# Second-half tokens turned by VectorE block transposes while they are normalized, and reloaded as channel-major rows

## The chip, the cores and the metric

The kernel runs on one core of one Trainium2 chip. The metric is the device time of one execution in microseconds (us); lower is better. TensorE is called PE below, VectorE DVE, ScalarE ACT, GpSimd POOL and SyncE SP, as in the profile.

## The reference

One layer of a hybrid decoder trunk for a sequence of 2048 tokens of 1024 channels, with 16 learned meta tokens put ahead of them. `h` is the RMS norm of the tokens, `p = h @ w_in` one projection to 8208 columns. Eight heads run a gated delta rule, and 1024 channels run a gated short convolution; both results are concatenated and projected back.

```python
def hybrid_layer(x, norm_g, w_in, ...):
    h = rmsnorm(x, norm_g)
    p = h @ w_in
    qkv, dn_z, dn_a, dn_b, sc_b, sc_c, sc_h, sc_z = jnp.split(p, SPLITS, axis=-1)
    qkv = jax.nn.silu(causal_dwconv(qkv, dn_conv_w))
...
    o = chunk_gated_delta_rule(q, k, v, g, beta)
    o = rmsnorm(o, dn_out_g) * jax.nn.silu(dn_z)
    y = sc_b * causal_dwconv(sc_c * sc_h, sc_conv_w)
    o_sc = y * jax.nn.silu(sc_z)
    return x + jnp.concatenate([o_dn, o_sc], axis=-1) @ w_out
```

The output is the RMS norm of the layer's result without the meta tokens.

## The kernel before, in words

**Halves.** The tokens are worked off in two halves of 1024. For each half the normalized tokens stand channel-major in two tiles, `hh` (`HH`, rounded to fp32r) and `hl` (`HL`, the rest), [128 channels, 8 channel groups, 1040 tokens]. There is one pair for both halves: a token tile of the second half (128 tokens) overwrites `hh` and `hl` when the last two projection jobs of the first half have passed those columns.

**Jobs.** A job (`run_group`, line 750) is one block of 128 output columns: 24 matmuls for each group of tokens (hh by wh, hl by wh, hh by wl), into the PSUM tile `mm`. The first half has three groups (272, 384 and 384 tokens), the second two of 512. A job's result is drained by ACT (`raw` and `acc` for the convolution of q, k and v) and finished by DVE (`acc<-raw,pcol,acc`). The weights of a later job are loaded by SP, rounded by ACT (`wh<-wr`), and their rest taken by DVE (`wl<-wr,wh`); for two jobs at the seam of the halves POOL takes the rest.

**Order.** PE, ACT, DVE and POOL run a fixed order written when the program is built. Jobs run one after the other; beside them run generators (streams) for the delta rule. A stream yields an amount of time, and `pump` (line 234) resumes it when a simple clock, kept by class `Model`, has passed that. So a stream's instructions fall between the matmuls of whatever job is running. Where a job needs something a stream has not delivered, `require` (line 257) advances the clock without emitting matmuls until the stream has. Engines run their lists strictly in order, and wait for one another by semaphores.

**A head.** For head `i` (0 to 7 in the first half, 8 to 15 in the second) `delta_front` (line 975) builds the blocks and runs a triangular substitution on DVE (`prod`, `XT`; `msm`, `mXT` for the meta tokens), `delta_back` (line 1124) merges blocks on PE (`ta`, tiles `Q`, `X`, `W`), and `delta_scan` (line 1304) runs eight chunks. Each chunk has three steps on PE, each waiting for the one before through another engine:

```python
mmf(pr[:, :128], lhsT=k_[:, c, :], rhs=S)        # rec<-S,k, then o<-S,qd
nc.vector.scalar_tensor_tensor(y, pr[:, :128], ...)   # DVE yy
mmf(pv[:, :128], lhsT=W[:, c, :], rhs=y)         # rec<-yy,W
nc.scalar.activation(vn, pv[:, :128], ...)       # ACT vn
mmf(pS[:, :128], lhsT=kd[:, c, :], rhs=vn)       # rec<-vn,kd, then o<-vn,P
nc.vector.scalar_tensor_tensor(Sn, S, ...)       # DVE S, then the next chunk
```

`delta_back(i)` waits for `("fresh", i)` and for scan `i - 1`. A job for k of head `i` needs scan `i - 2` (`pre_k`, line 830), a job for q needs the blocks of head `i - 2` (`pre_q`, line 836).

**The second half's tokens.** They are prepared during the first half. `normalize(t)` (line 526) loads tile t into `kd`, loads `norm_g` into the places of `Q` and `gw` (both held against other users meanwhile), takes the mean square on ACT and POOL, scales `kd` on DVE in two pieces of 128x512 and stores 512 KB to the DRAM tile `xnd`. It runs inside the stream `fresh(i)` (line 1079), after scan `i - 1`: one tile for heads 0 to 4 and 6, two for head 5. At the end of the first half `prologue1` (line 556) loads the eight tiles back into `sc_c`, `sc_y`, `sc_u`, and `turn` (line 391) does for each half tile four PE transposes into a PSUM tile `ta`, an ACT copy to `hh` and a DVE subtraction to `hl`. `LANDING` (line 1395) is the clock time given to a load.

## Time and profile before

| | |
|---|---|
| median of 3 runs | 2226.82 us (2225.97 to 2227.2) |
| the profiled execution, its own time | 2231.35 us |
| its span, first to last instruction | 2229.6 us |
| mean granted PE clock | 0.99 |
| busy share of the span | PE 98%, weight loads 86%, DVE 65%, ACT 38%, POOL 9% |
| DMA, mean over the span | 88 GB/s, 46% of the 16 engines' time |

The profile is of one execution. Views show the busy time of each engine in a stretch, the time that one engine waited for another, the instructions in order of time, and groups of equal instructions. A line is named by engine, operation, and output<-inputs with their sizes; all instructions stand at L118, the helper that records them, so tiles tell them apart. Transposes on PE are shown as MATMUL with `ident` as an input. A granted clock of 1.00 is 2.4 GHz, 0.50 is 1.2 GHz.

### The profile page before, as it was taken

To read this page: it belongs to the slowest core of one execution; us is meant where nothing else is said; L and a number is where in the kernel's file an instruction comes from. 1 tells how busy PE (TensorE), PEld (TensorE's weight loads), DVE (VectorE), ACT (ScalarE), POOL (GpSimd) and SP (SyncE) were. 2 spreads that over 40 slices of the span, in tenths; PEclk is the share of its full clock that TensorE was granted. 3 is DMA by queue.
4 is the path that set the end of the run, shared out by engine and by line. 5 is a ranking of instruction groups with operands and counts; after the bars stand their busy time and mean duration, and the time that the engine had idled before them with its cause. 6 is when DMAs were issued, how large, how long until landed. Compare 5 with 4: busy or idle time off the path is not lost.

```text
span 2229.6 us, 35449 instructions
## 1 busy us (share of the span) xinstructions
PE 2176.5 (98%) x13472; PEld 1917.2 (86%) x13472; DVE 1454.9 (65%) x3911; ACT 851.3 (38%) x1991; POOL 195.8 (9%) x361
## 2 busy tenths in 40 slices
PE   6999999999999999999999999999999999999998
PEld 5999999999999999878888888888878887788886
DVE  4677777777777777776767767676657683444222
ACT  5533434343434444443434352434342533322111
POOL 4010101010101010201010110010000100000000
PEclk9999999999999999999999999999989998999999
DMA  5434444353548844534254424353846443645321
GB/s 141 82 79 67 84 72 94 64 97 60 100 56 108 88 88 62 131 54 77 55 78 54 82 51 87 50 83 65 66 37 73 88 118 114 212 157 188 114 90 57
DMA packets 257096, 196.26 MB, mean 88 GB/s; under 512 B 61957, under 2 KB 226318, under 8 KB 256926
## 3 DMA queue, kind: packets, MB, share of 16 engines
q1 hardware_dynamic: 256926, 194.00, 46.0%
q8 instruction: 106, 1.74, 0.3%
q14 instruction: 64, 0.52, 0.1%
HBM read 157.89 MB, written 36.06 MB: 87 GB/s over the span
## 4 chain that ended last, share of the span: by engine, by line
PE 92%; DMA 2%; DVE 2%; ACT 2%; issue 1%; SPq 0%; POOLq 0%; ACTq 0%; DVEq 0%
PE mm L118 78%; PE ta L118 7%; PE rec L118 4%; PE o L118 3%; DMA wr<-in_w_in_dram 1%; ACT junk L118 1%; SPq L118 0%; DVE prod L118 0%; DVE hl L118 0%; DMA xtd<-XT 0%; DMA wr<-mixd 0%; DMA ysd<-raw 0%; DVE XT L118 0%; DVE acc L118 0%; ACT hh L118 0%
## 5 line engine op out<-in xcount | busy, mean ns | idle before, releaser
L118 PE MATMUL mm<-hh,wh 128*128 128x512 f32 (+3 forms) x2816 | 1006.3, 365 | 10.2 <-ACT hh L118 8.6
L118 PE MATMUL mm<-hl,wh 128*128 128x512 f32 (+3 forms) x2816 | 986.2, 358 | 0.2 <-DVE hl L118 0.2
L118 PE MATMUL mm<-hh,wl 128*128 128x512 f32 (+3 forms) x2816 | 641.4, 360 | 4.6 <-DVE wl L118 4.6
L118 PEld LDWEIGHTS mm<-hh,wh 128*128 128x128 f32 x2816 | 532.0, 190 | 61.5 <-ACT hh L118 9.8
L118 PEld LDWEIGHTS mm<-hl,wh 128*128 128x128 f32 x2816 | 531.9, 189 | 47.5 <-DVE hl L118 1.1
L118 PEld LDWEIGHTS mm<-hh,wl 128*128 128x128 f32 x2816 | 480.7, 189 | 53.6 <-DVE wl L118 5.5
L118 DVE TENSOR_TENSOR wl<-wr,wh 128x512 fp32r<-128x512 f32 x348 | 230.5, 685 | 69.3 <-ACT wh L118 34.1
L118 DVE SCALAR_TENSOR_TENSOR acc<-raw,pcol,acc 128x384 f32<-128x384 f32 (+2 forms) x360 | 231.3, 644 | 50.3 <-ACT acc L118 42.5
L118 ACT ACTIVATE wh<-wr 128x1024 fp32r<-128x1024 f32 x178 | 187.9, 1056 | 133.8 <-PE mm L118 88.1
L118 DVE SCALAR_TENSOR_TENSOR prod<-nb,XT 128x8 f32<-128x8 f32 (+30 forms) x496 | 194.3, 392 | 11.2 <-DMA nb<-nbd 6.4
L118 DVE TENSOR_REDUCE XT<-prod 128x8 f32<-128x16 f32 (+30 forms) x496 | 147.3, 297 | 17.1
L118 ACT ACTIVATE raw<-mm 128x384 f32<-128x384 f32 (+2 forms) x120 | 61.7, 514 | 227.8 <-PE mm L118 227.7
L118 ACT ACTIVATE vn<-rec,cj 128x128 f32<-128x128 f32 x128 | 46.9, 367 | 219.2 <-PE rec L118 218.8
L118 ACT ACTIVATE sc_c<-mm 128x384 f32<-128x384 f32 (+3 forms) x82 | 42.3, 516 | 176.1 <-PE mm L118 169.7
L118 PE MATMUL mm<-oh,wh 128*128 128x512 f32 x256 | 101.9, 398 | 0.0
L118 PE MATMUL mm<-ol,wh 128*128 128x512 f32 x256 | 100.4, 392 | 0.0
L118 DVE SCALAR_TENSOR_TENSOR yy<-rec,neg,vr 128x128 f32<-128x128 f32 x128 | 44.6, 349 | 71.6 <-PE rec L118 70.8
L118 DVE TENSOR_TENSOR y<-mm,y 128x512 f32<-128x512 f32 x23 | 15.9, 692 | 111.4 <-PE mm L118 111.4
L118 ACT ACTIVATE ojk<-y 128x512 bf16<-128x512 f32 x23 | 14.5, 631 | 183.4 <-DVE y L118 127.2
L118 POOL TENSOR_TENSOR opy<-mo,nhalf 128x4 f32<-128x4 f32 x32 | 33.7, 1052 | 509.4 <-DVE mo L118 509.4
L118 ACT ACTIVATE acc<-mm,pcol 128x384 f32<-128x384 f32 (+2 forms) x120 | 72.1, 601 | 0.1
L118 DVE SCALAR_TENSOR_TENSOR S<-S,egl,rec 128x128 f32<-128x128 f32 x104 | 35.8, 344 | 53.8 <-PE rec L118 53.5
(242 smaller groups left out, 2530.3 us busy)
## 6 DMA issues: line engine op xcount, KB each, us to landing
wr<-in_w_in_dram SPq DMA_DIRECT2D x128, 512.0 KB, 7.9
wr<-mixd SPq DMA_DIRECT2D x50, 512.0 KB, 4.5
E<-gtd SPq DMA_DIRECT2D x16, 512.0 KB, 3.8
qd<-ged SPq DMA_DIRECT2D x16, 512.0 KB, 3.9
nb<-nbd SPq DMA_DIRECT2D x64, 128.0 KB, 4.4
mixd<-zs SPq DMA_DIRECT2D x32, 256.0 KB, 2.4
out_dram<-y SPq DMA_DIRECT2D x16, 512.0 KB, 2.6
kd<-in_x_dram SPq DMA_DIRECT2D x9, 512.0 KB, 9.8
```

Of the source, the lines that this page charges most:

```text
L118: r = real(*args, **kw)
```

## The change

`normalize` does more. After each half tile of 128x512 is scaled, `turn_out` transposes its 32x32 blocks on DVE (one `STREAM_TRANSPOSE`, 128x512) into the place of the gain just used (`Q`, then `gw`), and four DMAs store it to `xnd`, which is now laid out by channel group, channel, token. Each writes rows of 32 elements (128 bytes) and 64 KB in all, so that the blocks land in their transposed positions. Then the stream yields `DRAIN` (4.0 on the order's clock) before `Q` and `gw` are let go and tile t is marked ready.

`prologue1` loads a tile as [128 channels, 8 groups, 128 tokens], rows of 512 bytes. `turn` with its PE transposes and its PSUM tile is gone; `split_h` copies from SBUF on ACT and subtracts on DVE, and the stream no longer waits for a `ta` slot.

```diff
-    xnd = tc.dram_tile([NC, 128, D], F32, name="xnd")
+    xnd = tc.dram_tile([NC, KT, 128, 128], F32, name="xnd")
...
-    def turn(xt, k0, col, n):
...
-            tr(pt[:, k, :n], xt[:, kx * 128 : kx * 128 + 128], n)
...
+    def split_h(xt, k0, col):
+        x_ = xt[:, 512 * k0 : 512 * k0 + 512].rearrange("p (k i) -> p k i", i=128)
+        h_ = HH[:, 4 * k0 : 4 * k0 + 4, col : col + 128]
+        l_ = HL[:, 4 * k0 : 4 * k0 + 4, col : col + 128]
+        nc.scalar.activation(h_, x_, AF.Copy)
+        nc.vector.tensor_tensor(out=l_, in0=x_, in1=h_, op=ALU.subtract)
...
             nc.vector.scalar_tensor_tensor(xc, xc, rs, gains[c2], op0=ALU.mult, op1=ALU.mult)
+            turn_out(
+                xnd[i, 4 * c2 : 4 * c2 + 4],
+                xc.rearrange("p (c i) -> p c i", i=128),
+                gains[c2].rearrange("p (c i) -> p c i", i=128),
+            )
+            yield after(eng="DVE", lag=0.3)
+        yield DRAIN
         held.discard("Q")
         held.discard("gw")
-        nc.sync.dma_start(xnd[i], xt)
...
-            nc.sync.dma_start(xts[i], xnd[i])
+            nc.sync.dma_start(
+                xts[i].rearrange("p (k i) -> p k i", i=128), xnd[i].rearrange("k p i -> p k i")
+            )
...
-                yield after(xts[i], slot=(pta, "ta"), eng="DVE", lag=1.2)
-                yield from hold()
-                turn(xts[i], k0, col, 128)
+                yield after(xts[i], eng="DVE", lag=1.2)
+                split_h(xts[i], k0, col)
...
+    def turn_out(dram, src, tmp):
+        nc.vector.transpose(out=tmp.rearrange("p c i -> p (c i)"), in_=src.rearrange("p c i -> p (c i)"))
+        for a in range(4):
+            nc.sync.dma_start(
+                dram[:, :, 32 * a : 32 * a + 32].rearrange("c (b y) x -> y (c b) x", b=4),
+                tmp[32 * a : 32 * a + 32].rearrange("y c (b x) -> y (c b) x", b=4),
+            )
...
+    DRAIN = 4.0
```

The instruction counts: PE loses 64 transposes, DVE gains 16 transposes, SP gains 56 DMAs (64 stores of 64 KB for 8 of 512 KB). All else is as often as before, but since the streams' yields differ, the instructions of the heads stand elsewhere among the jobs' matmuls. Two places follow.

**The end of head 4's scan, first on PE.** The last steps before, where `mm` rows are the running job:

```order
L118 MATMUL rec<-yy,W 128x128
L118 MATMUL mm<-hh,wh 128x384
L118 MATMUL mm<-hl,wh 128x384
L118 MATMUL mm<-hh,wl 128x384 x6
L118 MATMUL rec<-vn,kd 128x128
L118 MATMUL o<-vn,P 128x128
```

Eight matmuls of the job stood between the last two steps of the last chunk. The same steps on PE now:

```order
L118 MATMUL rec<-vn,kd 128x128
L118 MATMUL o<-vn,P 128x128
L118 MATMUL mm<-hh,wl 128x384 x2
L118 MATMUL rec<-S,k 128x128
L118 MATMUL o<-S,qd 128x128
L118 MATMUL rec<-yy,W 128x128
L118 MATMUL rec<-vn,kd 128x128
L118 MATMUL o<-vn,P 128x128
L118 MATMUL mm<-hh,wh 128x272
```

The chunk has moved back past the end of a job, so that its last two steps follow each other with none of a job's matmuls between them. The same place on ACT now:

```order
L118 ACTIVATE raw<-mm 128x384
L118 ACTIVATE acc<-mm,pcol 128x384
L118 ACTIVATE qcar<-raw 128x3
L118 ACTIVATE wh<-wr 128x1024
L118 ACTIVATE q<-acc 128x384
L118 ACTIVATE vn<-rec,cj 128x128
```

The last `vn` now stands behind the job's drain (`raw`, `acc`) and the rounding of the next weights (`wh`). Head 5 ends in the same way, with eight matmuls ahead of its last `rec<-S,k`.

**The end of head 6's scan, at the seam of the halves, on PE.** Before:

```order
L118 MATMUL rec<-S,k 128x128
L118 MATMUL o<-S,qd 128x128
L118 MATMUL mm<-hh,wl 128x384 x8
L118 MATMUL rec<-yy,W 128x128
L118 MATMUL mm<-hh,wh 128x384
```

These are the steps of the last chunk, inside the first half's last two jobs, with matmuls in every step. On PE now (the rows of 512 columns are the second half's first and second job):

```order
L118 MATMUL mm<-hh,wl 128x512 x5
L118 MATMUL rec<-yy,W 128x128
L118 MATMUL rec<-vn,kd 128x128
L118 MATMUL o<-vn,P 128x128
L118 MATMUL rec<-S,k 128x128
L118 MATMUL o<-S,qd 128x128
L118 MATMUL rec<-yy,W 128x128
L118 MATMUL rec<-vn,kd 128x128
L118 MATMUL o<-vn,P 128x128
L118 MATMUL mm<-hh,wh 128x512
```

The last four steps have moved behind the second half's first job and stand together, with no matmul of a job between them. DVE at this place now:

```order
L118 SCALAR_TENSOR_TENSOR yy<-rec,neg_857,vr 128x128
L118 TENSOR_TENSOR hl<-sc_c,hh 128x4x128
L118 SCALAR_TENSOR_TENSOR prod<-nb,XT 128x8x3
L118 TENSOR_REDUCE XT<-prod 128x8
L118 TENSOR_TENSOR hl<-sc_c,hh 128x4x128
L118 TENSOR_TENSOR hl<-sc_y,hh 128x4x128
L118 SCALAR_TENSOR_TENSOR prod<-nb,XT 128x8x4
L118 TENSOR_REDUCE XT<-prod 128x8
L118 TENSOR_TENSOR hl<-sc_y,hh 128x4x128
L118 SCALAR_TENSOR_TENSOR S<-S,egl,rec 128x128
```

The state `S` that the last chunk starts from has moved behind four subtractions for `hl` of the last two token tiles.

## Rows read from the trace of the kernel before

**Rows 1.** Page, part 1: busy us, share of the span, instructions.
```profile
PE 2176.5 (98%) x13472; PEld 1917.2 (86%) x13472; DVE 1454.9 (65%) x3911; ACT 851.3 (38%) x1991; POOL 195.8 (9%) x361
```

**Rows 2.** Time line of PE in the seam: start us, us, instruction.
```profile
910.25 0.34 PE L118 MATMUL mm<-hl,wh 128*128 128x384 f32 x1
910.43 0.60 PE L118 MATMUL ta<-ident,sc_c 128*128 128x128 f32 x4
910.78 0.42 PE L118 MATMUL mm<-hh,wh 128*128 128x384 f32 x1
911.04 0.33 PE L118 MATMUL mm<-hl,wh 128*128 128x384 f32 x1
```

**Rows 3.** Waits of PE: us in total, times, longest.
```profile
PE ta L118 <- DVE hl L118: 2.2, 2, 1.8
```

**Rows 4.** Windows: stretch, length, busy of PE, PEld, DVE, ACT, POOL; clock.
```profile
625.00:700.00 75.00, 74.95 (x596) 72.02 (x595) 52.52 (x156) 31.36 (x91) 7.50 (x14) 1.00 0.59 72
926.00:946.00 20.00, 16.95 (x93) 13.67 (x92) 19.26 (x61) 10.54 (x25) 8.07 (x8) 1.00 0.49 92
```

**Rows 5.** Time line of PE and ACT at the end of head 0's scan.
```profile
258.03 0.43 PE L118 MATMUL rec<-yy,W 128*128 128x128 f32 x2
...
258.23 0.49 ACT L118 ACTIVATE raw<-mm 128x384 f32<-128x384 f32 x1 [0.44 <-PE mm L118]
...
259.17 1.05 ACT L118 ACTIVATE wh<-wr 128x1024 fp32r<-128x1024 f32 x1
...
260.12 0.37 ACT L118 ACTIVATE vn<-rec,cj 128x128 f32<-128x128 f32 x1
...
260.54 0.49 PE L118 MATMUL rec<-vn,kd 128*128 128x128 f32 x2 [2.08 <-ACT vn L118]
```

**Rows 6.** Time line of two scan steps whose DVE and ACT stood free.
```profile
808.84 0.38 PE L118 MATMUL rec<-S,k 128*128 128x128 f32 x2
...
809.26 0.35 DVE L118 SCALAR_TENSOR_TENSOR yy<-rec,neg,vr 128x128 f32<-128x128 f32 x1 [0.37 <-PE rec L118]
...
810.69 0.38 PE L118 MATMUL rec<-yy,W 128*128 128x128 f32 x2
...
811.17 0.37 ACT L118 ACTIVATE vn<-rec,cj 128x128 f32<-128x128 f32 x1 [2.03 <-PE rec L118]
```

**Rows 7.** Groups of DVE by form: count, busy us, mean ns, idle before.
```profile
L118 DVE STREAM_TRANSPOSE X<-W 32x256 f32<-32x256 f32 x48 | 20.7, 432 | 11.8 <-DMA W<-xtd 10.8
L118 DVE TENSOR_TENSOR hl<-ta,hh 128x512 fp32r<-128x512 f32 x24 | 16.2, 683 | 4.7 <-ACT hh L118 4.4
...
L118 DVE SCALAR_TENSOR_TENSOR kd<-kd,pxr,Q 128x512 f32<-128x512 f32 x8 | 6.0, 752 | 0.4
```

**Rows 8.** Windows as in rows 4, around stalls of PE.
```profile
258.00:260.00 2.00, 0.46 (x4) 0.27 (x2) 1.08 (x6) 1.77 (x4) 0.00 (x0) 1.00 0.73 223
...
1620.00:1625.00 5.00, 4.10 (x41) 2.92 (x44) 3.65 (x7) 0.75 (x2) 0.00 (x0) 0.58 0.07 12
...
1635.00:1640.00 5.00, 5.00 (x21) 4.18 (x20) 1.01 (x2) 0.89 (x2) 0.00 (x0) 0.71 1.02 52
...
1840.00:1845.00 5.00, 1.45 (x5) 0.87 (x5) 2.02 (x4) 1.78 (x4) 0.00 (x0) 0.77 0.31 108
```

**Rows 9.** Time line of PE after a late weight in the output projection.
```profile
1932.91 2.08 PE L118 MATMUL mm<-hh,wl 128*128 128x512 f32 x4 [4.26 <-DVE wl L118]
1934.79 0.63 PE L118 MATMUL mm<-hh,wh 128*128 128x512 f32 x1
...
1938.20 0.44 PE L118 MATMUL mm<-hh,wh 128*128 128x512 f32 x1
...
1940.09 2.00 PE L118 MATMUL mm<-hh,wl 128*128 128x512 f32 x8
```

**Rows 10.** DMA issues: count, KB each, median us to landing.
```profile
wr<-in_w_in_dram SPq DMA_DIRECT2D x128, 512.0 KB, 7.9
...
nbd<-E SPq DMA_DIRECT2D x64, 32.0 KB, 2.4
```

More of the change, by code (lines that the diff above doesn't have):

```diff
@@ L388, in parted @@
         hready[hf, g] = max(model.free["ACT"], model.free["DVE"]) + model.LATENCY
-    def turn(xt, k0, col, n):
-        pt = ptile(pta, "ta", [128, 4, 128])
-        for k in range(4):
-            kx = 4 * k0 + k
-            tr(pt[:, k, :n], xt[:, kx * 128 : kx * 128 + 128], n)
-        h_ = HH[:, 4 * k0 : 4 * k0 + 4, col : col + n]
-        l_ = HL[:, 4 * k0 : 4 * k0 + 4, col : col + n]
-        nc.scalar.activation(h_, pt[:, :, :n], AF.Copy)
-        nc.vector.tensor_tensor(out=l_, in0=pt[:, :, :n], in1=h_, op=ALU.subtract)
+    def split_h(xt, k0, col):
[4 more added lines that the diff above has]
+        nc.vector.tensor_tensor(out=l_, in0=x_, in1=h_, op=ALU.subtract)
     def statistics(xt, n, jk):
```

## The prediction

> **What bounds the kernel now.** I read the busy shares first: PE is busy for 98% of the span, DVE for 65% [rows 1]. So PE's list of instructions sets the time, and only two things change it: matmuls taken from or added to that list, and time in which PE waits. The windows then tell where PE waits: in the middle of the first half it is busy for 74.95 of 75 us, while at the seam of the halves it is busy for 16.95 of 20 us and DVE for 19.26 [rows 4]. There DVE paces PE; one wait there is PE's transposes standing for `hl` to free their PSUM tile, 2.2 us [rows 3]. Last I read the time lines around the places where the change moves instructions. Idle time of DVE, ACT and SP elsewhere costs nothing.
>
> The sum is made against the profiled execution, 2231.35 us, whose span is 2229.6. The median of the runs is 2226.82, 4.5 lower, so I add the difference to the median. About 0.2%, 4.5 us, is what a measurement of this kernel can tell from no change.
>
> **The change, part by part.**
>
> *PE loses 64 transposes* (8 tiles, 8 each), in 16 groups of four. From one `hl` matmul over such a group to the next `hl` it takes 910.25 to 911.04 = 0.79 us; the same two matmuls without it would take two starts of 0.18, thus 0.35 [rows 2]. A group costs 0.44 us, 16 cost **7.0 us**.
>
> *The waits of the seam go:* 20 - 16.95 = 3.05 us of idle PE between 926 and 946 [rows 4], where the transposes waited for DVE. I take all of them out (**-3.05**) and put in below what PE waits for in their place.
>
> *DVE gains 16 transposes of 128x512.* The trace has only 32x256 ones, 0.43 us [rows 7]. The bounds are 0.43 (no cheaper than half as many columns) and 0.86 (twice that); the row of the same 128x512 size is the scaling's 0.75, which I take. 16 x 0.75 = 12 us on DVE, spread over the first half, where DVE has 22 of 75 us free [rows 4]: no cost. Without that cover it would be up to 0.86 each on the scan steps queued behind them (a rival below).
>
> *ACT and DVE at the seam:* the `hh` copies and `hl` subtractions (0.68 us each) stay as many, and read SBUF for PSUM [rows 7]: nothing. POOL gets nothing.
>
> *SP issues 64 stores for 8, and loads rows of 512 bytes.* A store of 32 KB in 128-byte rows lands after 2.4 us; a 512 KB load with 512-byte rows, as for the weights, after 7.9 [rows 10]. The stores stand on SP behind the DVE transposes and ahead of the next weight load; they are read again tens of us later, and the weights are fetched two jobs ahead. I cost both at nothing; one late weight load is the price if that cover goes (a rival below).
>
> *The order moves.* This is the larger part. `normalize` now yields longer (two pauses and `DRAIN`), so `delta_back` and the scan of heads 1 to 6 are emitted later, until the jobs that need a scan stand waiting for it. The order then holds scan steps with no job's matmuls between them: the end of head 4 (two), of head 5 (two), of head 6 (four). A bare step costs PE what the other engine needs. The trace has one, at head 0: 2.08 us, since `vn` stood behind `raw`, `acc` and the 1.05 us `wh` of a finished job [rows 5]. The floor is in two steps whose engines stood free: DVE starts 0.42 after the matmul and takes 0.35, ACT starts 0.48 after and takes 0.37 [rows 6]; with 0.05 until PE goes on (260.12 + 0.37 to 260.54 [rows 5]) a step takes 0.82 or 0.90 us. PE itself is busy for 0.36 of it where an `o` follows (0.14 behind a lone `rec<-yy`), so a bare step idles PE for 0.46 (`yy`, `S`) or 0.76 (`vn`) at least.
>
> - Head 4: `yy` 0.46. For `vn`, ACT's queue is that of head 0 with a further `q` (about 0.43): 258.23 to 260.12 = 1.89 from `raw` to `vn` [rows 5], 2.3 with `q`. `raw` starts about 1.0 (my estimate: `o`, two matmuls, their drain) after the previous `rec<-vn,kd`, so `vn` ends at 3.7 and PE, through at 1.8, idles 1.95. **+2.4.**
> - Head 5: the same queue behind eight more matmuls, **+2.4**.
> - Head 6, counted from its first bare `rec<-yy`: `vn` behind `raw` and `acc` idles PE 1.5. `S` stands behind the last two `hl` pieces, whose `hh` copies come on ACT after `vn`: 0.68 each with a substitution row between, so `S` ends at 4.35 and PE idles 2.4. `yy` behind a row and an `acc` of 128x512, 0.75 us like the scaling [rows 7]: 1.2. `vn`: 0.76. Together **+5.9**, within some 7 us.
>
> *The clock.* Granted TensorE clock fell to half, 1.2 GHz, in stretches where PE was busy for 1.45 of 5 us, or 4.10 of 5 in 41 short matmuls; at head 0, with 0.46 of 2 us busy, it stayed at 2.4 GHz [rows 8]. Head 6's stretch, about 1.4 us of matmuls in 7.3, is as empty as the first of these, so I count one fall there. With dense matmuls behind it, as at 1932.91, four matmuls took 1.88 us and the next eight 3.41, against 1.84 for eight at full clock behind 1940.09: (1.88 - 0.92) + (3.41 - 1.84) = **+2.5** [rows 9].
>
> Sum: -7.0 - 3.05 + 2.4 + 2.4 + 5.9 + 2.5 = **+3.2 us**: the profiled execution at 2234.5, the median at **2230.0**. What PE gives up in transposes comes back as bare scan steps.
>
> **The rivals.**
>
> *Faster: the bare steps stand at their floor and the clock stays.* If DVE and ACT have emptied their queues when the scan arrives, heads 4, 5 and 6 idle 1.2 + 1.2 + 2.4 = 4.9, and nothing falls: -10.05 + 4.9 = -5.15, **2221.7**. For it: head 0's gap left the clock alone [rows 8]. Against it: the queues are in the order, not a matter of chance.
>
> *Slower: the clock stays low for long.* After 1620 its mean is 0.58 in the first 5 us and 0.71 in 1635 to 1640 [rows 8], so, with the ten between them, it was at half for 4.2 + 10 + 2.9 = 17 us; with PE busy that loses up to 8.5 instead of 2.5. That gives +9.2, **2236.0**. It decides if what follows head 6 is sparse, or if heads 4 and 5 fall too. For it: that fall. Against it, that at 1932.91 ended after some 5 us of dense matmuls [rows 9], and behind head 6 stand 24 matmuls of 512 columns.
>
> *The change doesn't free what it says.* Six of the 16 transpose groups lie in the stretch where DVE is busy for 19.26 of 20 us [rows 4]. If DVE's work sets that stretch, taking 6 x 0.44 = 2.6 us from PE there gains nothing: +5.8, **2232.6**.
>
> *Slower: small stores hold up the weights.* Each tile puts 4096 rows of 128 bytes on the DMA queues ahead of a weight load. From the 2.4 us of a 32 KB store [rows 10] the bounds are nothing (all overlap) and 16 x 2.4 = 38 us per tile (none do), longer than two jobs. One late load costs the 4.26 us wait and the 2.5 us of clock seen at 1932.91 [rows 9]: +10, **2236.8**. The Trainium skill, in "DMA: Bandwidth & Descriptors", Specifications, asks for 512 bytes or more for line rate; by that these stores are the slow kind, and this case would be the likeliest. The trace's 128-byte stores, 2.4 us to landing four at a time, speak for overlap.
>
> *Slower: DVE's transposes delay the scan.* If each of the 16 stands ahead of a scan step and PE has no cover, 16 x 0.86 = 13.8 comes on top: **2243.8**. The Trainium skill, in "VectorE: DVE Perf Modes", Rules for kernel authors, says to transpose 128x128 on TensorE where a PSUM result will do, which speaks against this change. By rows, two 0.75 us scalings already stood together at each tile and PE lost 0.05 of 75 us in that stage [rows 4].
>
> **How the numbers follow.** Forecast 0.42 (its own range, from errors of some 3 us in bare steps and clock: 2226.5 to 2233.5), floor 0.20, long clock 0.20, seam paced by DVE 0.08, weights 0.06, DVE 0.04. Faster by over 0.2% needs under 2222.4: a good half of the floor case, 0.13, and a little of the forecast, 0.03, together 0.16. Slower needs over 2231.3: the four slower cases less their low sides, 0.34, and the upper tail of the forecast, 0.06, together 0.40. The rest, 0.44, is no change. The range, 2221 to 2238, takes in the floor, the long clock and one late weight load, and leaves out DVE and the outer halves of the others.
>
> **What would show it.** Right: no `ta<-ident,sc_` matmuls; PE waits `rec<-ACT vn` grown by some 5 us and `rec<-DVE` waits for `yy` and `S` new, at the ends of heads 4, 5 and 6; a granted clock under 1 just behind the seam; DVE transposes of 128x512 near 0.75 us, with no new PE wait in the rest of the first half. Wrong: PE idle at the seam under 3 us (floor), a low clock for over 10 us (long clock), PE waiting for `wl` or `wh` in the first half (weights), or waits of PE for DVE beside the transposes.

## The result, and the profile after

| | before | after |
|---|---|---|
| median of the runs | 2227.01 us (2225.97 to 2227.65, 4 runs) | 2255.59 us (2254.11 to 2259.03, 4 runs) |
| ratio to before | | 1.0121, 95% interval 1.0103 to 1.0139 |
| the profiled execution, its own time | 2231.35 us | 2254.11 us |
| its span | 2229.6 us | 2252.4 us |
| mean granted PE clock | 0.990 | 0.985 |

The change made the kernel 1.2% slower, some 28 us, where 2230.0 was forecast with no change as the likeliest outcome. The two profiled executions lie 22.8 us apart in time as in span, for 28.6 of the medians: that of before was a late one of its kernel, that of after an early one. The first part of the page after answers to [rows 1]:

```profile
PE 2181.0 (97%) x13408; PEld 1920.8 (85%) x13408; DVE 1455.1 (65%) x3927; ACT 849.6 (38%) x1991; POOL 193.4 (9%) x361
```

The 64 transposes have left PE (13472 instructions, now 13408), and yet PE is busy for 4.5 us more. If the 7.0 us of the prediction were taken out, matmuls took 11.5 us longer. The clock accounts for about as much: the span times the missing clock is 2229.6 x 0.010 = 22.3 us before and 2252.4 x 0.015 = 33.8 after, 11.5 more, though with a clock given to 0.001 each of the two is good to some 1 us. PE's idle time, span less busy, rose from 53.1 to 71.4 us, by 18.3. So the 22.8 us of longer span are 18.3 of waiting and 4.5 net of a lower clock. The waits of PE after (us in total, times, longest), the first of which answer to [rows 3]:

```profile
PE rec L118 <- ACT vn L118: 9.7, 7, 2.3
PE ta L118 <- DVE X L118: 9.2, 4, 8.0
...
PE o L118 <- ACT os L118: 5.0, 4, 1.7
...
PE rec L118 <- DVE S L118: 2.6, 2, 1.7
PE rec L118 <- DVE os L118: 2.1, 2, 1.9
```

The wait for `hl` of [rows 3] is gone. In its place stand waits for `vn`, `os` and `S`, at the ends of heads 4, 5 and 6 and at the seam, and one of 8.0 us for `X`, which the prediction did not have. Two more stand in the first half: 1.70 us for `os` at 579 us and 1.41 at 664.9, before a `ta` of `X` behind ACT's `wh`, which is most of what the first window below lacks to 75 us. The windows (columns as in [rows 4]) show the first stage of [rows 4], then the stretch around that wait, then head 6 at the seam:

```profile
625.00:700.00 75.00, 73.22 (x574) 70.64 (x573) 51.06 (x141) 29.68 (x79) 4.88 (x10) 1.00 0.64 63
...
775.00:780.00 5.00, 4.07 (x28) 3.72 (x26) 1.36 (x3) 3.13 (x10) 0.00 (x0) 1.00 1.07 112
780.00:785.00 5.00, 0.00 (x0) 0.00 (x0) 0.00 (x0) 0.00 (x0) 0.00 (x0) 0.92 0.73 133
785.00:790.00 5.00, 2.85 (x37) 2.68 (x38) 3.36 (x8) 0.75 (x2) 0.00 (x0) 0.50 0.25 69
790.00:795.00 5.00, 5.00 (x68) 4.54 (x66) 3.45 (x11) 2.42 (x5) 0.00 (x0) 0.56 0.03 7
...
956.00:960.00 4.00, 1.50 (x8) 0.82 (x6) 3.26 (x10) 2.47 (x5) 0.00 (x0) 1.00 0.82 137
960.00:965.00 5.00, 3.45 (x13) 2.78 (x14) 4.86 (x24) 1.40 (x3) 0.00 (x0) 0.66 0.43 127
```

From 780 to 785 no engine computes anything: all wait for a transfer. Behind it the clock stands at 1.2 GHz for about ten us, in part with PE fully busy. The chain of that wait, in the time line of SP, DVE and PE at head 5's `delta_back`:

```profile
766.91 0.44 SPq L118 DMA_DIRECT2D wr<-in_w_in_dram  x1
767.39 7.90 SPq L118 DMA_DIRECT2D xtd<-XT  x4
775.40 0.39 SPq L118 DMA_DIRECT2D wr<-in_w_in_dram  x1
775.89 5.18 SPq L118 DMA_DIRECT2D mixd<-sc_y  x1
781.25 1.85 SPq L118 DMA_DIRECT2D W<-xtd  x4
...
786.48 1.36 DVE L118 STREAM_TRANSPOSE X<-W 32x256 f32<-32x256 f32 x3 [9.96 <-DMA W<-xtd]
...
787.06 1.17 PE L118 MATMUL ta<-X,E 32*32 32x32 f32 x24 [7.99 <-DVE X L118]
```

Head 5's substitution result goes out to `xtd` and back into `W`. SP had issued the eight small stores of tile 6, head 5's second, by 766.8; a weight load followed, then `xtd`. SP needed 7.9 us to issue those four stores, and 5.18 for one store of `mixd` behind them, so the reload could only be issued at 781.25. The same steps before, in SP's time line:

```profile
741.32 0.38 SPq L118 DMA_DIRECT2D wr<-in_w_in_dram  x1
745.83 2.04 SPq L118 DMA_DIRECT2D xtd<-XT  x4
754.64 1.78 SPq L118 DMA_DIRECT2D W<-xtd  x4
```

There the round trip began 21.6 us earlier, with no small stores ahead of it (one store of 512 KB stood at 738.82), and PE had other work meanwhile. ACT's time line at head 4's last chunk shows a bare step, with the queue that the prediction read from [rows 5]:

```profile
714.85 0.49 ACT L118 ACTIVATE raw<-mm 128x384 f32<-128x384 f32 x1 [1.75 <-PE mm L118]
...
715.79 1.06 ACT L118 ACTIVATE wh<-wr 128x1024 fp32r<-128x1024 f32 x1
716.74 0.52 ACT L118 ACTIVATE q<-acc 128x384 f32<-128x384 f32 x1
717.15 0.37 ACT L118 ACTIVATE vn<-rec,cj 128x128 f32<-128x128 f32 x1
```

For the experiments one measure is used throughout: when the Nth of the job matmuls (`mm`, 9296 in every kernel) starts, against the profiled execution of before, in us. A scan that stands elsewhere moves such a number for a while; the 4300th lies between the ends of heads 5 and 6, the 5200th behind the seam.

| kernel (profiled execution) | 3700th | 4300th | 5200th | 7000th | 9200th |
|---|---|---|---|---|---|
| the change | +5.8 | +19.2 | +22.5 | +21.9 | +22.7 |
| no_turn_one_store | +1.0 | +5.5 | +6.4 | +6.0 | -0.3 |
| small_stores_no_turn | +3.0 | +15.0 | +13.9 | +15.1 | +14.7 |
| turn_one_store | +7.7 | +12.1 | +17.1 | +19.5 | +15.2 |
| tiles_01_at_head0 | +9.9 | +14.3 | +25.7 | +25.1 | +21.5 |
| xtd_other_queue | +7.3 | +20.2 | +23.1 | +22.5 | +15.4 |
| turn_not_in_the_order | +2.5 | +10.0 | +10.0 | +9.6 | +3.8 |
| same_order_large_stores | +5.5 | +9.9 | +10.6 | +10.2 | +9.7 |
| same_order_no_turn | +9.6 | +13.6 | +18.8 | +18.4 | +20.2 |
| no_turn_short_hold | +1.4 | +6.6 | +13.2 | +17.0 | +11.2 |
| no_turn_4096_wl_dve | +2.1 | +5.1 | +9.5 | +13.4 | +4.7 |
| no_turn_tile_first | +2.6 | +7.6 | +6.5 | +10.3 | -0.7 |

### The profile page after: what moved, and what is told of

It reads as the page before. It is cut to its first block, busy times and chain, and to the rows that moved or that the text cites. A ratio compares the mean times of both kernels' runs of the same rounds, so it can differ in the third digit from the quotient of the medians.

```text
span 2252.4 us, 35382 instructions
## 1 busy us (share of the span) xinstructions
PE 2181.0 (97%) x13408; PEld 1920.8 (85%) x13408; DVE 1455.1 (65%) x3927; ACT 849.6 (38%) x1991; POOL 193.4 (9%) x361
## 4 chain that ended last, share of the span: by engine, by line
PE 87%; DMA 4%; DVE 4%; ACT 2%; SPq 1%; issue 1%; POOL 0%; POOLq 0%; ACTq 0%; DVEq 0%
PE mm L118 74%; PE ta L118 6%; PE rec L118 4%; PE o L118 2%; SPq L118 1%; DMA wr<-in_w_in_dram 1%; DMA W<-xtd 1%; DVE prod L118 1%; ACT junk L118 1%; DMA xtd<-XT 1%; DMA nb<-nbd 1%; DVE XT L118 0%; DMA sc_y<-xnd 0%; DVE wl L118 0%; DVE sc_y L118 0%
## 5 line engine op out<-in xcount | busy, mean ns | idle before, releaser
L118 DVE SCALAR_TENSOR_TENSOR prod<-nb,XT 128x8 f32<-128x8 f32 (+30 forms) x496 | 193.7, 390 | 18.4 <-DMA nb<-nbd 14.8
L118 DVE TENSOR_TENSOR y<-mm,y 128x512 f32<-128x512 f32 x23 | 15.9, 692 | 111.8 <-PE mm L118 111.8
L118 ACT ACTIVATE ojk<-y 128x512 bf16<-128x512 f32 x23 | 14.5, 631 | 183.4 <-DVE y L118 127.2
```

Of the source, the lines that this page charges most:

```text
L118: r = real(*args, **kw)
```

## The experiments

**Which part costs it.** Each of the first three keeps the longer yields and drops the transposes, the small stores, or both.

*no_turn_one_store*

```diff
-            turn_out(...)
...
+        nc.sync.dma_start(xnd[i].rearrange("k p i -> p k i"), xt.rearrange("p (k i) -> p k i", i=128))
```

> The changed kernel without the 16 DVE transposes and with one store of 512 KB per tile in place of the eight small ones; the longer yields and the copy from SBUF stay, and so does the removal of the 64 PE transposes. The tokens of the second half are therefore not turned. PE's list has no bare scan step at heads 4 to 6 and head 5 still takes two tiles. Theory A (the loss is in the order of the instructions: bare scan steps, the 8 us wait for W<-xtd, and clock falls behind both): 7.0 us of transposes and the 3.05 us of seam idle come off in full, about 2217 us against 2227. Theory B (the 64 small stores and their place on SP): also about 2217. Theory C (the transposes' time on DVE): also about 2217. If it is 2222 or more, the gain from PE was priced too high, and the loss of 28 us is smaller than thought.

Measured: 2232.96 us, ratio 1.0023 (1.0008 to 1.0038). Without transposes on any engine and without small stores the kernel is not faster than before. So the -7.0 and -3.05 of the sum don't arrive in the time; this became the second question.

*small_stores_no_turn*: `turn_out` without its transpose, its stores reading `xc`.

> The changed kernel with its 64 small stores (64 KB each, rows of 128 bytes) reading the scaled half tiles directly; only the 16 DVE transposes are left out, so the blocks are not turned. PE's list again has no bare scan step at heads 4 to 6. Theory A (order): within 3 us of the run without small stores, about 2217 to 2220. Theory B (small stores hold up the xtd round trip and the weights): most of the 28 us that the change lost stay, 2240 or more, with the wait of PE for X behind W<-xtd of some 8 us. Theory C (DVE transposes): about 2217.

Measured: 2246.03 us, 1.0079 (1.0055 to 1.0104). With no bare steps, PE waits 5.8 us for `X` at head 5, and is 15.0 us behind at the 4300th job matmul where the run above is 5.5. That speaks for a part of theory B, but the two differ in order too: their traces show the same list of PE up to 747 us, and from there on, in head 5's blocks, another one, although the expectation has PE's list without bare steps in both. Two runs below separate order and stores better.

*turn_one_store*: the transposes as they are, one store of 512 KB for the eight.

> The changed kernel with its 16 DVE transposes, but the stores of the small kind replaced by one store of 512 KB of the unturned tile. On PE's list the bare scan steps of heads 4 (two), 5 (one) and 6 (one) are back, without the four of head 6. Theory A (order): about 2217 plus bare steps of 1.5 to 2 us each at heads 4, 5, 6 and one clock fall, 2222 to 2228; if the X wait of head 5 also comes back, some 10 us more. Theory B (small stores): about 2217. Theory C (transposes on DVE): within 5 us of the changed kernel, 2250 or more.

Measured: 2245.45 us, 1.0078 (1.0049 to 1.0106). More than theory A's 2228, less than C's 2250. There is no long wait for `X`; bare steps of 1.5 to 1.9 us at heads 4 to 6 are followed by falls of the clock.

*tiles_01_at_head0*

```diff
-            news = ((0,), (1,), (2,), (3,), (4,), (5, 6), (7,), ())[i] if hf == 0 else ()
+            news = ((0, 1), (2,), (3,), (4,), (5,), (6,), (7,), ())[i] if hf == 0 else ()
```

> The changed kernel with one edit in the table of tiles: head 0 normalizes two tiles (0, 1), heads 1 to 6 one each, so head 5 no longer has two. All transposes and small stores stay. PE's list has no bare scan step at heads 4 to 6, but three at head 0 where the first kernel had one. Theory A (order): 2227 - 10 + some 3 for head 0 = about 2220, no X wait of several us in the middle of the first half. Theory B (small stores): the weights and xtd still stand behind the stores, so 2240 or more. Theory C (transposes on DVE): 2240 or more.

Measured: 2251.59 us, 1.0106 (1.0079 to 1.0133). The bare steps of heads 4 to 6 and the long `X` wait are gone, and nothing is gained: at head 0 it falls from 2.4 us behind at the 900th job matmul to 9.0 at the 1300th, and waits of 5.0 and 2.7 us for `S` and 6.1 for `os` stand at the seam. My theory A fell in its simple form, that bare steps are the loss.

**The order and the queue.**

*xtd_other_queue*

```diff
-                nc.sync.dma_start(
+                (nc.queue2 if i == 5 else nc.sync).dma_start(
                     xtd[i % 2, 8 * q : 8 * q + 8].rearrange("m p i -> p m i"), XT[32 * q : 32 * q + 32]
```

and the same for `W<-xtd`; `queue2` is POOL.

> The changed kernel with one edit: for head 5 the four stores xtd<-XT and the four loads W<-xtd are issued by POOL instead of SP. PE, ACT and DVE keep their lists word for word. Theory B1 (the 8 us wait of PE for X is the round trip through xtd standing behind a weight load on SP's queue): the wait for X at head 5 falls under 2 us and the clock fall behind it goes (4.6 us), so 2243 to 2246 against 2255.6. Theory B2 (the DMA engines themselves are full, whichever queue issues): the wait stays at 6 us or more and the time within 2 us of 2255.

Measured: 2248.44 us, 1.0087 (1.0063 to 1.0111), but not for the reason of B1. POOL's and PE's time line:

```profile
772.22 2.31 POOL L118 DMA_DIRECT2D W<-xtd  x4
785.86 0.43 DVE L118 STREAM_TRANSPOSE X<-W 32x256 f32<-32x256 f32 x1 [7.87 <-DMA W<-xtd]
786.44 0.28 PE L118 MATMUL ta<-X,E 32*32 32x32 f32 x2 [5.88 <-DVE X L118]
788.09 1.06 PE L118 MATMUL ta<-X,E 32*32 32x32 f32 x30 [1.37 <-DVE X L118]
```

The reload was issued 9 us earlier, took 13.6 us in place of 5.2, and PE waited 5.88 + 1.37 us. At the 5200th job matmul nothing was gained (+23.1 and +22.5); the 7 us appear behind the 7000th, where a fall of the clock was shorter. So B2: the DMA engines are full there (their share is 0.98 and 1.02 in the two windows from 770 to 780 in this trace, and 1.07 from 775 to 780 in the change's). POOL's queue itself is not the slow one: in turn_not_in_order_xtd the same four loads, issued by POOL for heads 0, 2, 3 and 4, landed after 1.95 to 2.2 us. The Trainium skill says the same in "DMA: Bandwidth & Descriptors", Issuing engines are not separate DMA queues: whichever engine starts a DMA, it runs on the same 16 DMA engines. This trace agrees, with 13.6 us.

*turn_not_in_the_order*

```diff
-        nc.vector.transpose(out=tmp.rearrange(...), in_=src.rearrange(...))
+        tc.nc.vector.transpose(out=tmp.rearrange(...), in_=src.rearrange(...))
```

> The changed kernel, all of its computation and DMAs, but the 16 transposes are not shown to the clock that sets the order. PE's list is then that of the run without transposes and with one store (no bare scan steps at heads 4 to 6). Theory A (the transposes cost by the order that they bring about): DVE's 16 x 0.71 us themselves cost nothing, so this run lies within 3 us of the run with small stores and no transposes (2246). Theory C (the transposes delay what stands behind them on DVE): 10 us or more above it, 2256 or more. Theory B (small stores cost some 13 us): it stays 10 us or more above the run with one store (2233).

Measured: 2235.98 us, 1.0033 (1.0018 to 1.0049). The same computation and transfers as the change, 20 us faster by its order alone. It stands 0.0010, 2 us, over no_turn_one_store, whose PE list it shares, so transposes and small stores together cost little in this order. Theory C's 2256 is out; so is a fixed price of the small stores. Theory A's number failed as well: this run should have come within 3 us of small_stores_no_turn, and is 10 us faster, with the same stores and the transposes on top. The two differ in PE's list, so the 10 us between them came by the order. What the stores cost depends on what they stand ahead of.

*turn_not_in_order_xtd*: the same, `xtd` and `W` of the first half's eight heads through POOL.

> As the run before it in this set, with xtd<-XT and W<-xtd of all eight heads of the first half issued by POOL. If B1 is right for both kernels: the X wait of head 5 (5.8 us in the run with small stores and no transposes) and the clock fall behind it (4 us) go, so 2233 to 2237, level with the run with one store. By B2: no change from the run before it in this set.

Measured: 2262.29 us, 1.0149 (1.0124 to 1.0174), the slowest of all. PE waits 3.75, 5.0 and 6.9 us before `ta` matmuls at 209, 774 and 1020 us. Neither theory has this. The trace shows what it is at the first two places; POOL's and ACT's time line at 774:

```profile
772.88 2.30 POOL L118 DMA_DIRECT2D W<-xtd  x4 [15.45 <-PE ta L118]
...
776.44 1.06 ACT L118 ACTIVATE E<-E 128x1024 f32<-128x1024 f32 x1 [9.60 <-POOL E L118]
```

POOL runs its list in order, and the reload stands in it until it can be issued. POOL's own work on `E` comes behind it, and ACT, and through ACT PE, waits for that: 9.60 us here, 5.21 at 208. At 1020 PE waits for `X`, whose reload, issued at 1018.62, landed after 7.0 to 8.3 us.

*no_turn_short_hold*: no_turn_one_store without the three added yields.

```diff
-            yield after(eng="DVE", lag=0.3)
-        yield DRAIN
```

> As the run without transposes and with one store, but also without the three added yields: the stream lets Q and gw go at once, as in the first kernel. The tokens are not turned. PE's list is that of the first kernel up to the seam of the halves; behind that the 64 transposes are missing. Theory A (the longer hold of Q and gw costs some 5 us in the middle of the first half, where that run stood 5.5 us behind at its 4300th job matmul): under 1 us behind there, and 5 us faster than that run in all, 2222 to 2228. Theory D (the seam is paced by DVE, so that taking 7.0 us of transposes from PE gains little there): at the seam, from the 4300th to the 5200th job matmul, no more than 3 us are gained. Rival to D: the seam gains the 10 us that were forecast, 2217.

Measured: 2242.47 us, 1.0055 (1.0034 to 1.0076). With the first kernel's order the middle of the first half is no better (+6.6 at the 4300th), so the longer hold does not cost 5 us. And the seam loses 6.6 us more. Both of A's numbers failed; D's "under 3 us gained" held, by far.

**The change's own order, one part left out.** Here PE's list is the change's, word for word.

*same_order_large_stores*

```diff
-        for a in range(4):
-            nc.sync.dma_start(dram[:, :, 32 * a : 32 * a + 32].rearrange(...), tmp[32 * a : 32 * a + 32].rearrange(...))
+        for a in range(4):
+            model.issue("DMA", nc.sync.cost("dma_start", [d_], [s_], (), {}), [d_], [s_])
+        tc.nc.sync.dma_start(dram.rearrange("k p i -> p k i"), tmp)
```

> The changed kernel with PE's, ACT's and DVE's lists kept word for word (the four small stores are still counted by the clock that sets the order), but what SP issues in their place is one store of 256 KB per half tile, rows of 512 bytes. The tokens are block-transposed, and their blocks are not put in place. Theory B (small stores on SP and the DMA engines make W<-xtd of head 5 late): the wait of PE for X there, 8.0 us, falls under 3 us, the clock fall behind it (4.6 us) goes, 2240 to 2246. Theory A (the order alone makes that wait): it stays at 6 to 9 us and the time within 3 us of 2255. The bare scan steps of heads 4, 5 and 6 stay in either case (some 9 us of idle PE).

Measured: 2241.40 us, 1.0049 (1.0032 to 1.0067). PE's waits there:

```profile
PE ta L118 <- DVE X L118: 1.3, 4, 0.6
```

From 9.2 us to 1.3, and the time falls by 0.0072 x 2227 = 16 us. Theory B as predicted: in this order the small stores make `W<-xtd` late. How they do so stands in the time lines of SP and ACT, first of the change:

```profile
737.66 2.00 SPq L118 DMA_DIRECT2D xnd<-gw  x4
741.73 0.39 SPq L118 DMA_DIRECT2D wr<-in_w_in_dram  x1
742.16 0.58 SPq L118 DMA_DIRECT2D kd<-in_x_dram  x1
...
756.74 0.63 ACT L118 ACTIVATE gw<-kd 128x512 bf16<-128x512 f32 x1 [13.81 <-DMA kd<-in_x_dram]
```

and then SP's of this kernel:

```profile
737.40 0.36 SPq L603 DMA_DIRECT2D xnd<-gw  x1
737.85 0.46 SPq L118 DMA_DIRECT2D kd<-in_x_dram  x1
...
741.48 4.25 SPq L118 DMA_DIRECT2D wr<-in_w_in_dram  x2
```

Here the load of tile 6 is issued ahead of the next weights and lands after 4.2 us. In the change it is issued 0.43 us behind a weight load and lands after 14.5, so the tile is scaled 4.0 us later (760.15 for 756.18), `XT` ends 4.0 us later, and `xtd`, behind the next small stores and a further weight load, is issued 8.4 us later (767.39 for 758.99). The small stores of head 5 are not slow themselves: where the trace has their landing, it is 1.75 to 3.8 us after the issue. SP's list is not one of those that the program fixes, and it differs between the two kernels in where weight loads stand; no run changes the stores' size and keeps SP's list. What stays, 11 us over before, is bare steps, the new waits at the seam and the clock.

*same_order_no_turn*: as the change, the transposes counted by the clock but not emitted.

> The changed kernel with PE's and ACT's lists kept word for word and its 64 small stores, but without the 16 DVE transposes (they are still counted by the clock that sets the order). What is stored is the gain that stood in the place of the turned tokens. Theory C (the transposes' 11.4 us on DVE cost time themselves): 2245 or less. Theory A (what they cost comes by the order): within 3 us of the changed kernel, 2252 to 2258.

Measured: 2246.88 us, 1.0079 (1.0061 to 1.0096), between both theories. Here too the `X` wait is gone (2.2 us in all). Both edits move head 5's round trip out of its place behind a weight load: `xtd` is issued at 762.66 here, ahead of the next weights at 768.37. The two savings, 16 and 9 us, contain the same wait and do not add. And the 9 us are not shown to be DVE's work: what is stored here is the gain, which does not wait for the scaled tokens, so the first stores of tile 6 are issued at 741.90 for 761.67 in the change. The profiled execution was the slowest, 2251.5, and shows only 2.5 of the 9.

**Why PE's saved time did not arrive.** The rest looks at the seam.

*turn_free_wl_on_dve*: turn_not_in_the_order, with `wl` of the seam's two jobs on DVE.

```diff
-            eng.tensor_tensor(out=J.wl, in0=J.wr, in1=J.wh, op=ALU.subtract)
+            for s_ in (slice(0, 4), slice(4, 8)):
+                tc.nc.vector.tensor_tensor(out=J.wl[:, s_], in0=J.wr[:, s_], in1=J.wh[:, s_], op=ALU.subtract)
```

> The kernel whose order doesn't count the transposes, with one further edit: wl<-wr,wh of the two jobs at the seam goes from POOL (one instruction of 128x1024) to DVE (two of 128x512 each, 0.7 us apiece); PE's list is unchanged. In the run before, hl<-sc_y,hh and hl<-sc_u,hh took 2.53 and 2.44 us in place of 0.69 just while POOL worked on that wl. Theory E (DVE and POOL get in each other's way where both operands stand in SBUF): no hl over 0.75 us, the wait rec<-ident,os behind DVE os falls from 6.5 us by 0.5 to 1 us (3.6 us of stretching goes, 2.8 us of wl come), 2233 to 2236 against 2236. Rival (chance overlap, the stretching has another cause): the two hl stay near 2.4 us and the time rises by some 3 us, 2239.

It came from these rows of no_turn_one_store's time line:

```profile
930.72 2.40 POOL L118 TENSOR_TENSOR wl<-wr,wh 128x1024 fp32r<-128x1024 f32 x1 [9.45 <-ACT wh L118]
931.14 2.53 DVE L118 TENSOR_TENSOR hl<-sc_y,hh 128x512 fp32r<-128x512 f32 x1 [1.71 <-ACT hh L118]
936.89 2.38 POOL L118 TENSOR_TENSOR wl<-wr,wh 128x1024 fp32r<-128x1024 f32 x1 [1.73 <-ACT wh L118]
937.36 2.45 DVE L118 TENSOR_TENSOR hl<-sc_u,hh 128x512 fp32r<-128x512 f32 x1 [0.99 <-ACT hh L118]
```

Measured: 2235.36 us, 1.0025 (1.0015 to 1.0035). All 16 `hl` took 0.67 to 0.69 us, and the wait for `os` fell from 6.5 to 4.8. Theory E holds; the time is level.

*turn_free_tiles_12*: that kernel, with tiles (0), (1, 2), (3) to (7) for heads 0 to 6.

> As the run before it in this set, but the second tile of head 5 goes to head 1: heads 0 to 7 take (0), (1, 2), (3), (4), (5), (6), (7) and none; PE's list has no bare scan step at heads 4 to 6. If the waits around 750 to 790 us (1.6 and 2.1 us of idle PE with a clock fall of 1.7 us, and 10 us behind the first kernel at the 4300th job matmul) come from head 5's two tiles, these go: 2226 to 2230, level with the first kernel or faster. If they come from the small stores or the transposes wherever they stand, they move to head 1's place and the time is within 3 us of the run before it.

Measured: 2237.13 us, 1.0039 (1.0022 to 1.0056). The place of the two tiles is not the cause: PE is 15.9 us behind at the 4300th.

*no_turn_rows_4096*: no_turn_short_hold with the first kernel's layout of `xnd`.

> The run with the short hold and no transposes anywhere (2242 us), with one edit: store and loads have the first kernel's layout, rows of 4096 bytes. The tokens are not turned. PE's list is unchanged. If the 512-byte rows slow the weights around 740 to 780 (PE waited 2.42 us for wl there, and the clock fell): that wait goes, at the 4300th job matmul it stands within 1 us of the first kernel, 2235 to 2238. If not: within 2 us of 2242. If the seam is paced by DVE, it still gains under 3 us between the 4300th and the 5200th job matmul; if the sum of the prediction was right there, it gains 10 and comes to 2219.

Measured: 2235.81 us, 1.0024 (1.0012 to 1.0036). The wait around 773 stayed (2.48 us), so the rows of 512 bytes are not its cause; nor is it one for `wl`, as my expectation said, but one for nothing that the profile names (last section). At the 4300th job matmul it is 4.1 us behind in place of 6.6, but the run with 512-byte rows has two falls of the clock, at 261 and 776, that this one lacks. The seam loses 5.8. The time is 7 us lower all the same; in the profiled executions that comes behind the 7000th job matmul, where one fall of the clock is shorter.

*no_turn_4096_wl_dve*: that kernel, `wl` of the seam on DVE.

> As the run before it in this set, with wl of the two jobs at the seam on DVE instead of POOL; PE's list is unchanged. In the run with the short hold one hl took 2.26 us beside POOL's wl. If that stretching matters, the seam gains 1 to 2 us more; if DVE's load there matters, it loses as much.

Measured: 2232.78 us, 1.0014 (1.0001 to 1.0026). This trace has the answer. From the 4300th to the 4700th job matmul PE goes from 5.1 us behind to 5.2 ahead: the 10 us of the sum are there. Then SP's, ACT's and DVE's time line:

```profile
928.26 0.38 SPq L118 DMA_DIRECT2D wr<-in_w_in_dram  x1
928.82 0.44 SPq L118 DMA_DIRECT2D sc_y<-xnd  x1
...
940.63 1.16 ACT L118 ACTIVATE hh<-sc_y 128x512 fp32r<-128x512 f32 x2 [6.37 <-DMA sc_y<-xnd]
941.30 0.69 DVE L118 TENSOR_TENSOR hl<-sc_y,hh 128x512 fp32r<-128x512 f32 x1 [4.16 <-ACT hh L118]
```

The last token tile's load, 0.56 us behind a weight load on SP, is used 11.8 us later. ACT and then DVE stand for it, `os` is behind `hl` in DVE's list, and PE waits 6.8 us for `os`; some 2.5 us more go at 1.2 GHz behind it (granted clock 0.76 from 950 to 960, with PE busy throughout). The 10 us are lost again. The first kernel has no such wait. Its time line of PE and SP, and DVE's of this kernel, show why that load comes later here:

```profile
922.43 0.66 PE L118 MATMUL ta<-ident,sc_y 128*128 128x128 f32 x4
923.12 0.32 SPq L118 DMA_DIRECT2D sc_y<-xnd  x1
```

```profile
928.11 0.68 DVE L118 TENSOR_TENSOR hl<-sc_y,hh 128x512 fp32r<-128x512 f32 x1
```

The load writes the place of an earlier tile. With PE's transposes that place was free once PE had read it, at 923.09, and the load was issued 0.03 us later, with the next weight load only at 930.16. Without them ACT and DVE read the tile itself, the place is free when DVE's `hl` ends at 928.79, and the load, again 0.03 us later, stands behind a weight load.

*turn_gather_on_load*: stores of the turned half tiles as they stand, loads that pick the blocks.

```diff
+            for b in range(4):
+                nc.sync.dma_start(
+                    xts[i][32 * b : 32 * b + 32].rearrange("y (c a x) -> y c a x", a=4, x=32),
+                    xnd[i].rearrange("(a y) (c b x) -> b y c a x", a=4, b=4, x=32)[b],
+                )
```

> All of the computation: the DVE transposes stay (not counted in the order), each half tile is stored as it stands, in one store of 256 KB with rows of 2048 bytes, and the loads at the seam pick the blocks in 128-byte pieces (four loads of 128 KB per tile); wl of the seam on DVE. If the small pieces hurt because they fall in the stretch of full DMA engines around 740 to 780: that stretch gets faster by 3 to 5 us and the time falls to 2228 to 2232. Rival: the 4096 pieces per tile land too late at the seam, where hh waits for them: 5 to 15 us slower, 2240 to 2250.

Measured: 2238.44 us, 1.0043 (1.0027 to 1.0060). The stretch around 760 hardly improves (+9.3 at the 4300th, for +10.0 and +13.0 in the two kernels of this order with the small stores), and waits of 1.0 us for `wh` and 1.1 for `hh` stand at the seam.

*turn_gather_short_hold*: that kernel without the added yields.

> As the run before it in this set, without the three added yields (Q and gw are let go at once on the order's clock, the semaphores still guard them). PE's list is the first kernel's up to the seam. By theory A, which has longer holds shift the heads: up to 3 us faster than the run before it; if the hold matters nothing, level with it.

Measured: 2245.80 us, 1.0072 (1.0055 to 1.0089). Again the shorter hold is slower.

*no_turn_tile_first*

```diff
...
             J.wr = vt(wp, [128, KT, 128], "wr")
+            if gate is not None:
+                tc.nc.gpsimd.tensor_copy(J.wr[:1, 0, :1], gate[:1, :1])
```

with `gate` the last token tile.

> The run without transposes, rows of 4096 bytes and wl on DVE (2232.8 us), with one edit: the weight load that stood on SP just ahead of the last token tile's load now waits until that tile has landed (a copy of one element on POOL makes it wait). The tokens are not turned. If that load is what holds ACT, DVE and with them os: the load lands within 4 us, the wait for os falls from 6.8 us to under 3, with no clock fall behind it, 2223 to 2227, faster than the first kernel. If DVE's own work sets os: the wait stays over 5 us and the time within 2 us of 2233.

Measured: 2228.43 us, 0.9994 (0.9982 to 1.0006). The wait for `os` fell from 6.78 us to 2.61, as expected. From the 4300th to the 5200th job matmul the kernel now gains 1.1 us where the run without the edit lost 4.4. So the load was the cause of that wait's larger part. The time missed its 2223 to 2227: 2.6 us of wait for `os`, 2.7 us behind it at 996, and the clock falls behind each, are what comes next.

*turn_tile_first*: turn_free_wl_on_dve with the same edit.

> All of the computation: the kernel whose order doesn't count the transposes, wl of the seam on DVE (2235.4 us), with the same single edit. If the token tile's load is what holds os: the wait of 4.8 us for os falls under 2.5 and the clock fall behind it (1.7 us) goes, 2230 to 2233; it would still be behind the first kernel by what the small stores cost at head 5. If DVE's work sets os: within 2 us of 2235.

Measured: 2235.14 us, 1.0026 (1.0015 to 1.0037). The wait for `os` stayed at 4.8: in this order it is DVE's own list that holds `os`, as the rival had it. No version with the whole computation beat the first kernel.

## Why the prediction was wrong

- *The order.* That bare scan steps would appear at the ends of heads 4, 5 and 6 was right, and for the reason given. Their sizes were over-priced: 0.22 + 1.47 us at head 4 and 0.22 + 1.60 at head 5 for 2.4 each, and at head 6, in PE's time line, 4.05 in all for 5.9:

```profile
957.93 0.49 PE L118 MATMUL rec<-vn,kd 128*128 128x128 f32 x2 [1.14 <-ACT vn L118]
960.38 0.49 PE L118 MATMUL rec<-S,k 128*128 128x128 f32 x2 [1.74 <-DVE S L118]
961.74 0.80 PE L118 MATMUL rec<-yy,W 128*128 128x128 f32 x2 [0.65 <-DVE yy L118]
963.05 0.80 PE L118 MATMUL rec<-vn,kd 128*128 128x128 f32 x2 [0.52 <-ACT vn L118]
```

- *The step that failed first: "SP issues 64 stores for 8 ... I cost both at nothing".* In the change's order they cost 16 us (same_order_large_stores, with what SP's list changes beside them). The stores take their place on SP, 2.0 us for four where one large store takes 0.36, and a tile's load and then `xtd` fell behind weight loads. I looked at what reads the stored data and at the weights, and not at the small round trip `xtd` that the same shift of the order carried behind them. The rival "small stores hold up the weights" had the mechanism and a price of 10, with a chance of 0.06; the transfer held up was another one. The Trainium skill's rule cited there, "DMA: Bandwidth & Descriptors", Specifications, would have made it the likeliest case, and the time went that way. But the trace does not show slow stores behind it (1.75 to 3.8 us to landing at head 5), and by turn_not_in_the_order, 1.0033, the same stores cost almost nothing where nothing urgent follows them.
- *The seam: "I take all of them out (-3.05)", and the -7.0.* Of the 3.05 only 2.2 were waits of the transposes; 0.77 was one for `os`. In no_turn_4096_wl_dve PE did get the 10 us, and gave them back at the next thing that was late: the token tile's load, then DVE's `os`. The load is late by a term that the sum puts at nothing, that `hh` and `hl` "read SBUF for PSUM": it holds the tile's place until DVE is through. In the change itself new waits of 2.27 us for `vn` and 1.18 and 1.90 for `os` stand between 924 and 950. The rival "seam paced by DVE" was half of it. A stall taken out of a sum has to be followed by asking what is late next; I asked that only for head 6.
- *The clock: "I count one fall".* Before 1000 us the first kernel has none; the change has four, behind 2.07 us of idle at 261, the 8.0 at 779, the 2.27 at 925 and head 6. These four last 23.9 us together, which with PE busy costs half of that, 12 us for the 2.5 of the sum; the falls behind 1600 us are about 4 us shorter than before. That idle of 2.07 us at head 0 was in [rows 5] and left the clock at 2.4 GHz [rows 8]; the same wait in the change was followed by 1.2 GHz. So one row without a fall does not show that there is a margin.
- *DVE's transposes.* They took 0.711 us for the forecast 0.75:

```profile
L118 DVE STREAM_TRANSPOSE gw<-kd 128x512 f32<-128x512 f32 x8 | 5.7, 711 | 0.3
```

That they cost nothing as work is borne out by turn_not_in_the_order; what they cost comes by the order and by where the stores then fall.

Of the added waiting, 18.3 us net, the longest piece is the 8.0 at head 5; the bare steps of heads 4 to 6 are 7.6, where 10.7 were forecast, the three new waits at the seam 5.4, the two at 579 and 665 us 3.1, and some 6 us of the first kernel's waits are gone. The signs that the prediction named for being right came, but for its last, "no new PE wait in the rest of the first half". Open is how long a fall of the clock lasts around 1630 to 1660: the change and xtd_other_queue, with one and the same PE list, come out 8 us apart behind the 7000th job matmul (the last two columns of the table), and no run here settles why.

## What to carry to other kernels

A transfer that was issued right behind a large load landed, or was used, 10 to 15 us later here, with 32 KB as with 512 KB, and a small one from POOL's queue, with the DMA engines full, fared the same; so when a change moves a stream, list every transfer that it issues and look in the new trace at what stands ahead of each. Where a tile is read by another engine than before, ask when its place comes free. Work taken off the bounding engine is worth what is left until the next thing is late: find that thing in the trace before counting the gain. And where a clock of the builder sets the order, a kernel in which the new instructions are not counted by that clock tells the price of the order from the price of the work.

## What was not expected of the hardware

- DVE's subtraction of 128x512 with both inputs in SBUF took 2.45 and 2.53 us in place of 0.69 while POOL ran a subtraction of its own on SBUF, and ended 0.55 us behind POOL's; with POOL's work gone all took 0.67 to 0.69. The prediction put "read SBUF for PSUM" at nothing. The Trainium skill has this in "SBUF — State Buffer", SBUF: two separate sides: an instruction of DVE with two SBUF inputs and one of POOL that reads SBUF share a port pair that one holds for its whole length. The rows agree. In the change itself no `hl` met POOL's `wl`, but two small instructions of DVE did: `opt<-opy` took 2.35 us at 945.72 in place of some 0.14, and `prod<-nb,XT` 2.29 at 951.08 in place of 0.17. The first kernel has two as well (2.37 and 2.00 us), so this is no part of what the change cost; but `os`, for which PE waits 1.90 us in the change, stands right behind the first of them.
- PE stood 2.69 us in no_turn_4096_wl_dve for nothing that a semaphore shows. PE's time line, and the packets of the DMA queues from 772.5 to 776:

```profile
775.63 0.34 PE L118 MATMUL mm<-hl,wh 128*128 128x384 f32 x1 [2.69 <-issue]
```

```profile
q8 instruction: 1, 0.02, 1.7%
```

From 760 to 773 the DMA engines were busy for 92.1% and no packet of instructions came; one came inside the wait. Waits of 2.1 to 4.3 us of this kind stand between 771 and 782 in nine of the kernels here, and none in the first kernel or the change. In all nine traces a packet of instructions ended 1.2 to 1.5 us before PE went on. In the five kernels with neither transposes nor small stores the wait, with the fall of the clock where one follows, is over half of what they lose ahead of the 4300th job matmul. That full DMA engines make PE's instructions late is what this suggests; no run took it apart.
